# A two-layer hybrid decoder trunk: transposes kept together, up blocks taken two at a time, and the first loads and last stores on two queues

## The chip, the cores and the metric

The kernel runs on one NeuronCore of a Trainium2 chip. The core has a matrix engine (TensorE, PE in the profile, with its weight loads as PEld), a vector engine (VectorE, DVE), a scalar engine (ScalarE, ACT), a general engine (GpSimd, POOL) and a sequencer that only issues transfers (SyncE, SP). Each runs its own stream of instructions in order; semaphores tie the streams together. Matrix results land in PSUM, eight banks of 128 x 512 float32, and DVE or ACT take them from there to SBUF. Transfers between HBM and SBUF are issued by an engine's sequencer onto a queue and carried by 16 DMA engines.

The metric is the device time of one execution in microseconds; lower is better. Timed runs give a median, and one further execution is profiled.

## What is computed

Two layers. In each, a normalised copy of the tokens (256 x 1024) is projected, eight heads of sparse attention and eight heads of forgetting attention run side by side, their result is projected back, and a squared-ReLU MLP follows. Cut to what matters here:

```python
for l in range(DEPTH):                                   # DEPTH = 2
    h = _rms_norm(x, g_pre_mix[l])
    parts = jnp.split(h @ w_in[l], split_at, axis=-1)    # 1024 -> 2848 columns
    o_nsa = _nsa_mixer(...)                              # 8 heads, three branches
    o_fox = _fox_mixer(...)                              # 8 heads
    mix = jnp.concatenate([o_nsa, o_fox], axis=-1) @ w_out[l]
    x = x + _rms_norm(mix, g_post_mix[l])
    h = _rms_norm(x, g_pre_mlp[l])
    y = jnp.square(jax.nn.relu(h @ w_up[l])) @ w_down[l]  # 1024 -> 4096 -> 1024
    x = x + _rms_norm(y, g_post_mlp[l])
```

## The kernel before

**Products in three parts.** A float32 product is made of three products of rounded halves: each operand is split into `hi` (rounded to the type float32r) and `lo` (the rest), and hi*hi, hi*lo and lo*hi are summed in one PSUM bank (`mm3`, L657). The weights come from HBM as float32 into a buffer `wraw` (tag `raw`, 9 buffers), ACT makes `whi` from it and DVE `wlo` (`Weights.get`, L485; 7 buffers of each). So each weight tile of 512 KB costs one load, one ACT instruction and one DVE instruction, and then feeds PE.

**Transposes.** PE also turns blocks of 128 x 128 by a product with the identity (`ident`, a column range of the tile `cst`). These are plain float32. The profile shows them as `s<-cst,...`: `pr` are attention probabilities (`probs_T`, L1215), `mg` the normalised tokens (`to_xT`, L694), `kS` and `kW` keys (`k_transpose`, L865), `h` the first MLP block (`turn`, L1450). Each group of three or four writes one bank with the tag `s`; there are three such banks, two each with the tags `x` and `acc`, and one with the tag `o`.

**Small-tile stretches.** Some attention products use a part of the PE array: the forgetting scores (`s<-fkT,fqT` and `s<-cum,selr`, 64 rows), probability times value (`o<-prT,...`, 64 columns) and the hidden layer of the compressed keys (32 columns). They are recorded inside `nc.stretch()`, which makes one unit of several matmuls.

**The order is planned.** `body` does not issue instructions as the code runs. A `Recorder` collects every operation with its buffers, dependencies and an estimated cost (`_cost`, L446; `_latency`, L423). `order` (L282) then makes a list schedule, five times with due times worked out from the last one, keeps the one that ends first by its own estimate, and `emit` issues the instructions in that order. All instructions thus carry the line L404 in the profile, and groups are told apart by tile names. Outside a stretch the planner is free to put other matmuls between two transposes of one group; inside a stretch it is not. An operation on `sync` counts as a transfer in these estimates (L271, L368, L424, L451).

**The MLP.** Layer by layer, `up(fc)` (L1403) makes 512 of the 4096 hidden columns, transposed, in four blocks `b` of 128. For each block, eight matmuls with `whi` as the stationary operand read 512 columns (both halves of the tokens `xT`, tile `xT[2]`), then eight with `wlo` read 256 columns (the half `xT[0]`), all into one bank of tag `s`. ACT copies the second half of the bank to `h`, DVE adds the first half, and after every second block the squared ReLU is taken and split into the two halves of `aT`. `up` runs for `fc` 1 to 7 in each layer (14 times in all); each is followed by the `down` products of the block before (four weight tiles, 48 matmuls into banks `x` and `acc`). `up0` (L1431) makes the first block in another layout.

**The beginning.** The first eight loads (L598 to L611) each bring one tile `first`: 128 rows with 256 columns of the transposed tokens and 512 of the first weights, 384 KB (388 KB with the gains in front of the first). All are issued by SyncE. `ACT_TABLE_LOAD` (L517) is ACT's first instruction. For each `k`, ACT scales the tokens to `xT` and rounds the weights to `whi` (DVE for `k` = 0), DVE makes both `lo` parts, and PE does six matmuls of 512 columns into the two banks `x`. Before the first load lands, PE runs four warm-up matmuls (`o<-warm`).

**The end.** `sandwich` (L710) of each token tile `t` normalises the down product and adds it to `X[t]`, in two halves of 512 columns; in the last layer each half is stored by SyncE as soon as DVE has written it (L748).

Of the kernel before, what the change touches and what calls it, by code (L numbers as in the profile page):

```python
# [24 lines left out]
P = 128  # L25
D = 1024
S = 256
# [150 lines left out]
class Recorder:  # L178
# [75 lines left out]
    def deadlines(self, out):  # L254


        due, t = {}, 0.0
        for op in out:
            if op.engine == "tensor":
                due[op], t = t, t + op.cost  # L260
        taker = {}
        for q in self.fifo.values():
            for a, b in zip(q, q[q[0].bufs:]):
                taker[a] = b
        first = {}
        for op in out:
            for b in op.bufs:
                first.setdefault(b, op)
        for op in reversed(out):
            d = due.get(op, t)  # L270
            cost = op.cost + LANDING if op.engine == "sync" else op.cost  # L271
            for x in op.succs:
                if x.deps[op] > -1e8 and x in due:
                    d = min(d, due[x] - x.deps[op] - cost)
            for b in op.bufs:
                if taker.get(b) in first and first[taker[b]] in due:
                    d = min(d, due[first[taker[b]]] - (260 if b.psum else 150) - cost)
            due[op] = d
        for op in out:
            op.rank = op.key if op.engine == "tensor" else due[op]  # L280
# [16 lines left out]
    def schedule(self):  # L297
# [41 lines left out]
        while events:  # L339
            t, _, released = heapq.heappop(events)  # L340
            if released is not None:
                free[released] += 1
            if events and events[0][0] == t:
                continue
            for e, ops in waiting.items():
                while busy[e] <= t:
                    best = None
                    for op in ops:
                        if op.ready <= t and (best is None or (best.urgent, -best.rank) < (op.urgent, -op.rank)) and fits(op):
                            best = op  # L350
                    if best is None:
                        break
                    if not best.urgent and e != "tensor" and not force:
                        q = hot[e]
                        while q and q[0].start is not None:
                            q.popleft()
                        memo = {}
                        if any(estimate(op, memo) < t + WAIT * best.cost for op in list(q)[:4] if op.start is None and fits(op)):
                            break
                    ops.remove(best)  # L360
                    for b in best.bufs:
                        if b not in live:
                            live.add(b)
                            free[b.tag] -= 1
                            head[b.tag] += 1
                    best.start = t
                    out.append(best)
                    if e == "sync":  # L368
                        busy[e] = t + 450
                        bus = max(bus, t + 1150) + best.cost  # L370
                        best.end = bus + 900 + LATE
                    else:
                        busy[e] = best.end = t + best.cost
                        if e == "tensor" and best.tile != tiled:
                            busy[e] = best.end = best.end + (tiled == (P, P)) * ENTER + (tiled != (P, P)) * LEAVE
                            tiled = best.tile
                    count += 1
                    heapq.heappush(events, (busy[e], count, None))
                    for b in best.bufs:
                        left[b] -= 1  # L380
                        if not left[b]:
                            count += 1
                            heapq.heappush(events, (best.end + (260 if b.psum else 150), count, b.tag))
                    for s in best.succs:
                        s.ready = max(s.ready, t, best.end + s.deps[best])
                        s.missing -= 1
                        if not s.missing:
                            waiting[s.engine].append(s)
                            count += 1
                            heapq.heappush(events, (s.ready, count, None))  # L390
            force = not events and len(out) < len(self.ops)
            if force:
                heapq.heappush(events, (t + 100, 0, None))
# [27 lines left out]


def _latency(a, b):  # L423
    if a.engine == "sync":  # L424
        return 50.0
    if a.engine == b.engine == "tensor":
        return 0.0
    if a.engine == "tensor":
        return 360.0 if b.name == "tensor_tensor_reduce" else 200.0
    if b.engine == "tensor":  # L430
        return 260.0 if a.engine == "vector" else 230.0
    return 130.0 if a.engine == "vector" else 145.0
# [13 lines left out]
def _cost(op, views):  # L446
# [1 line left out]
    out = op.args[0] if op.args else op.kw["out"]  # L448
    n = int(np.prod(out.shape[1:]))
    part = 100 * (out.shape[0] < P)  # L450
    if op.engine == "sync":  # L451
        v = views[0][1]
        return v.shape[0] * int(np.prod(v.shape[1:])) * 4 / 360.0
    if op.engine == "tensor":
# [68 lines left out]
def trunk(nc, A, consts_in, out, sbp, pp):  # L523
# [6 lines left out]
    def small(shape, name, bufs=2):  # L530
        return tile(shape, F32, name=name, tag=name, bufs=bufs)
# [50 lines left out]
    def weight(*key):  # L582
        return W.get(index[key])
# [13 lines left out]
    for k in range(8):  # L597
# [6 lines left out]
        o = 0 if k else 8  # L604
        f = f[:, 0:o + NFIRST]
        a = 8 + k * NFIRST - o
        nc.sync.dma_start(f, A["first"][:, a:a + o + NFIRST])
        if k == 0:
            gcol0 = f[:, 0:8]
        xTk.append(f[:, o:o + S])  # L610
# [83 lines left out]
    def to_xT(t, n, xg, xT):  # L694

        ps = psum("s")
        for k in range(4):
            nc.tensor.transpose(ps[:, k * P:k * P + P], xg[:, k * P:k * P + P], ident)
        split(ps.rearrange("p (k n) -> p k n", k=4), [y[:, 4 * n:4 * n + 4, t * P:t * P + P] for y in xT[:2]])

    def pre_gain(g_post, g_next):
# [8 lines left out]
    def sandwich(t, acc, g_post, pre=None, xT=None, eps=EPS, store=None):  # L710
# [32 lines left out]
        for n in range(2):  # L743
            if pre:
                m[n] = times("m", n, g_post)
            nc.vector.scalar_tensor_tensor(X[t][:, half(n)], m[n], r, X[t][:, half(n)],
                                           op0=OP.mult, op1=OP.add)
            if store is not None:  # L748
                nc.sync.dma_start(store[:, half(n)], X[t][:, half(n)])
        yield  # L750

    def rope(dst, src, t, nh):
# [31 lines left out]
    for l in range(DEPTH):  # L784
# [80 lines left out]
        def k_transpose(br, src):  # L865

            ps = psum("s")
            for g in range(2):
                for t in range(NT):
                    nc.tensor.transpose(ps[:, g * S + t * P:g * S + t * P + P], src[t][:, g * P:g * P + P], ident)  # L870
            split(ps.rearrange("p (g n) -> p g n", g=2), [y[:, :, br, :] for y in kx])


# [340 lines left out]

        def probs_T(p, eng, e):  # L1215
            ps = psum("s")
            for a in (0, 128, 256):
                nc.tensor.transpose(ps[:, a:a + P], p[:, a:a + P], ident)
            kind, pair, par, br = e
            if kind == "nsa" and pair % 2:  # L1220

# [180 lines left out]

        def up(fc, then=None):  # L1403
            a = [tile([P, 4, S], F32R, name="aT", tag=f"act{j}", bufs=2) for j in range(2)]
            for b in range(4):
                hi, lo = weight(l, "up", fc, b)

                ps = psum("s")
                for k in range(8):
                    nc.tensor.matmul(ps, hi[:, k, :], xT[2][:, k].rearrange("p j n -> p (j n)"), start=k == 0, stop=False,  # L1410
                                     skip_group_check=True)
                for k in range(8):
                    nc.tensor.matmul(ps[:, S:], lo[:, k, :], xT[0][:, k, :], start=False, stop=k == 7,
                                     skip_group_check=True)
                if then is not None and b == 1:
                    then()
                if b % 2 == 0:
                    h = tokt("h")
                d = h[:, (b % 2) * S:(b % 2) * S + S]
                nc.scalar.activation(d, ps[:, S:], AF.Copy)  # L1420
                nc.vector.tensor_add(d, ps[:, :S], d)
                if b % 2:
                    rl = small([P, 512], "rl")
                    nc.scalar.activation(rl, h, AF.Relu)
                    nc.vector.tensor_mul(h, rl, rl)
                    d = [y[:, b - 1:b + 1, :].rearrange("p b n -> p (b n)") for y in a]
                    nc.scalar.activation(d[0], rl, AF.Square)
                    nc.vector.tensor_sub(d[1], h, d[0].bitcast(F32))
            return a

        def up0():  # L1431
# [127 lines left out]
```

## Time and profile before

| | us |
|---|---|
| median of 3 runs (lowest, highest) | 623.21 (622.92, 623.8) |
| the profiled execution, whole time | 622.97 |
| its span, first to last instruction | 621.0 |
| PE busy in it | 613.3 |
| DVE busy | 476.3 |
| ACT busy | 376.3 |

The span lies 2.0 us below the time of its own execution. The mean granted TensorE clock of the profiled run was 0.999 of full speed. A row of the timeline gives the start of a group, how long it lasted from its first start to its last end, the engine, the line, the operation, what is written from what, and the count. Matmuls overlap in a pipeline, so the time that one takes of the engine is the distance to the start of the next, not its own duration. Rows of the chain of waits give the start, the length and the instructions of a piece of the work that ended last.

### The profile page before, as it was taken

The page shows a single profiled execution, that of the slowest core. Times are in us where ns is not written, and L with a number is a line of the kernel's source. Part 1 is how long each engine was busy: PE and PEld are TensorE (multiplying, and loading weights), DVE is VectorE, ACT ScalarE, POOL GpSimd, SP SyncE. Part 2 cuts the span into 40 slices and gives each one's busy share as a digit, 9 for nine tenths or more (in the row PEclk, how much of TensorE's full clock was granted, in tenths as well). Part 3 has the DMA queues.
Part 4 walks back from the last instruction along what each step waited for, and adds up shares of the span by engine and source line. Part 5 has one row for each costly group of instructions (what it writes and reads, how often), then busy time and mean ns, then how long its engine had stood idle before and what let it go on. Part 6 is the DMA issues. An engine that isn't in the chain of part 4 may idle for free.

```text
span 621.0 us, 9923 instructions
## 1 busy us (share of the span) xinstructions
PE 613.3 (99%) x3572; PEld 518.0 (83%) x3572; DVE 476.3 (77%) x1043; ACT 376.3 (61%) x730; POOL 0.2 (0%) x4
## 2 busy tenths in 40 slices
PE   9999999999999999999999999999999999999995
PEld 6989987788888888888888998777888888888884
DVE  6889999789966567566698999987997666566544
ACT  7866777577655455555476758774766555556432
POOL 0000000000000000000000000000000000000000
PEclk9999999999999999999999999999999999999999
DMA  8987636218665546654347793521485556556001
GB/s 317 403 311 277 257 111 218 73 41 306 245 199 203 195 177 201 203 172 135 111 128 255 269 332 103 174 98 69 132 306 204 175 196 196 193 183 202 12 1 68
DMA packets 33600, 115.69 MB, mean 186 GB/s; under 512 B 3984, under 2 KB 4112, under 8 KB 33552
## 3 DMA queue, kind: packets, MB, share of 16 engines
q1 hardware_dynamic: 33552, 115.06, 53.4%
q8 instruction: 28, 0.46, 0.3%
q14 instruction: 20, 0.16, 0.1%
HBM read 114.00 MB, written 1.05 MB: 185 GB/s over the span
## 4 chain that ended last, share of the span: by engine, by line
PE 99%; DVE 0%; issue 0%; DVEq 0%; ACT 0%
PE s L404 35%; PE acc L404 31%; PE x L404 25%; PE o L404 7%; DVE x L404 0%; DVE m L404 0%; DVEq L1555 0%; DVE rsqrt L404 0%; DVE warm L404 0%; ACT rl L404 0%; DVEq L404 0%
## 5 line engine op out<-in xcount | busy, mean ns | idle before, releaser
L404 DVE TENSOR_TENSOR wlo<-wraw,whi 128x1024 fp32r<-128x1024 f32 (+1 forms) x188 | 224.8, 1201 | 80.5 <-ACT whi L404 78.6
L404 ACT ACTIVATE whi<-wraw 128x1024 fp32r<-128x1024 f32 (+1 forms) x188 | 194.8, 1040 | 122.1 <-PE acc L404 72.8
L404 PE MATMUL s<-xT,whi 128*128 128x512 f32 x448 | 112.0, 392 | 0.0
L404 PEld LDWEIGHTS s<-xT,whi 128*128 128x128 f32 x448 | 81.4, 189 | 15.2
L404 PE MATMUL acc<-whi,aT 128*128 128x512 f32 x256 | 88.6, 390 | 0.0
L404 PE MATMUL x<-whi,aT 128*128 128x512 f32 x256 | 88.4, 390 | 0.0
L404 PEld LDWEIGHTS s<-xT,wlo 128*128 128x128 f32 x448 | 61.1, 190 | 4.4
L404 PE MATMUL s<-xT,wlo 128*128 128x256 f32 x448 | 62.5, 282 | 0.0
L404 PEld LDWEIGHTS acc<-whi,aT 128*128 128x128 f32 x256 | 48.1, 188 | 9.9
L404 PEld LDWEIGHTS x<-whi,aT 128*128 128x128 f32 x256 | 48.1, 188 | 9.7
L404 ACT ACTIVATE pr<-pr,st 128x256 f32<-128x256 f32 (+1 forms) x96 | 42.8, 448 | 15.2 <-DVE st L404 14.7
L404 PE MATMUL x<-wlo,aT 128*128 128x512 f32 x128 | 50.0, 390 | 0.0
L404 PE MATMUL acc<-wlo,aT 128*128 128x512 f32 x128 | 49.9, 390 | 0.0
L404 PE MATMUL acc<-xT,whi 128*128 128x256 f32 x256 | 49.7, 288 | 0.0
L404 PEld LDWEIGHTS acc<-xT,whi 128*128 128x128 f32 x256 | 40.2, 190 | 1.6 <-issue 0.4
L404 PE MATMUL acc<-whi,xT 128*128 128x512 f32 (+1 forms) x128 | 38.8, 361 | 0.0
L404 ACT ACTIVATE rl<-h 128x512 f32<-128x512 f32 x28 | 17.7, 632 | 32.5 <-DVE h L404 32.5
L404 PE MATMUL acc<-xT,wlo 128*128 128x256 f32 x128 | 36.6, 286 | 0.0
L404 PE MATMUL x<-whi,xT 128*128 128x512 f32 x112 | 36.3, 397 | 0.0
L404 DVE TENSOR_TENSOR h<-rl 128x512 f32<-128x512 f32 x28 | 19.2, 691 | 16.1 <-ACT rl L404 16.1
L404 PEld LDWEIGHTS acc<-wlo,aT 128*128 128x128 f32 x128 | 24.0, 188 | 5.0
L404 PEld LDWEIGHTS x<-wlo,aT 128*128 128x128 f32 x128 | 24.1, 188 | 4.5
(221 smaller groups left out, 961.9 us busy)
## 6 DMA issues: line engine op xcount, KB each, us to landing
wraw<-in_w_up_dram SPq DMA_DIRECT2D x64, 512.0 KB, 4.2
wraw<-in_w_down_dram SPq DMA_DIRECT2D x64, 512.0 KB, 3.5
wraw<-in_w_in_dram SPq DMA_DIRECT2D x36, 512.0 KB, 4.9
wraw<-in_w_out_dram SPq DMA_DIRECT2D x16, 512.0 KB, 7.7
w<-in_cmp_w_k_dram SPq DMA_DIRECT2D x8, 512.0 KB, 5.8
w<-in_cmp_w_v_dram SPq DMA_DIRECT2D x8, 512.0 KB, 5.3
first<-in_first_dram SPq DMA_DIRECT2D x7, 384.0 KB, 5.9
wraw<-in_w_in_dram SPq DMA_DIRECT2D x8, 288.0 KB, 4.2
```

Of the source, the lines that this page charges most:

```text
L404: getattr(getattr(self.nc, op.engine), name)(*[real(v) for v in args], **{k: real(v) for k, v in kw.items()})
```

## The change

Four things change, and one in the planner that goes with them.

1. The transposes of `to_xT`, `k_transpose` and `probs_T` are recorded inside `nc.stretch()`, so that the three or four of a group stand together and start when all that they read is there.
2. In `up`, blocks go by two: both weights are taken, then come the 16 matmuls with `whi` (eight into each of two banks), then the 16 with `wlo`, then the evacuation of both banks.
3. The first two loads (`k` 0 and 1) are each cut into rows 0 to 63, issued by SyncE, and rows 64 to 127, issued by ACT.
4. The last half of the last token tile is written by DVE in two pieces of 320 and 192 columns; ACT's queue stores the first, SyncE's the second.
5. The planner knows a transfer by its name instead of by its engine.

```diff
-            cost = op.cost + LANDING if op.engine == "sync" else op.cost
+            cost = op.cost + LANDING if op.name == "dma_start" else op.cost
...
-        nc.sync.dma_start(f, A["first"][:, a:a + o + NFIRST])
+        if k < 2:
+            for q, h in ((nc.sync, slice(0, HD)), (nc.scalar, slice(HD, P))):
+                q.dma_start(f[h], A["first"][h, a:a + o + NFIRST])
+        else:
+            nc.sync.dma_start(f, A["first"][:, a:a + o + NFIRST])
...
-        for k in range(4):
-            nc.tensor.transpose(ps[:, k * P:k * P + P], xg[:, k * P:k * P + P], ident)
+        with nc.stretch():
+            for k in range(4):
+                nc.tensor.transpose(ps[:, k * P:k * P + P], xg[:, k * P:k * P + P], ident)
...
-            nc.vector.scalar_tensor_tensor(X[t][:, half(n)], m[n], r, X[t][:, half(n)],
-                                           op0=OP.mult, op1=OP.add)
-            if store is not None:
-                nc.sync.dma_start(store[:, half(n)], X[t][:, half(n)])
+            for a, b in ((0, 512),) if store is None or t == 0 or n == 0 else ((0, 320), (320, 512)):
+                d = X[t][:, n * 512 + a:n * 512 + b]
+                nc.vector.scalar_tensor_tensor(d, m[n][:, a:b], r, d, op0=OP.mult, op1=OP.add)
+                if store is not None:
+                    (nc.scalar if a == 0 and b < 512 else nc.sync).dma_start(store[:, n * 512 + a:n * 512 + b], d)
...
-            for b in range(4):
-                hi, lo = weight(l, "up", fc, b)
-                ps = psum("s")
-                for k in range(8):
-                    nc.tensor.matmul(ps, hi[:, k, :], xT[2][:, k].rearrange("p j n -> p (j n)"), start=k == 0, stop=False,
-                                     skip_group_check=True)
-                for k in range(8):
-                    nc.tensor.matmul(ps[:, S:], lo[:, k, :], xT[0][:, k, :], start=False, stop=k == 7,
-                                     skip_group_check=True)
+            for b in (0, 2):
+                ws = [weight(l, "up", fc, b + i) for i in range(2)]
+                two = [psum("s") for _ in range(2)]
+                for ps, (hi, _) in zip(two, ws):
+                    for k in range(8):
+                        nc.tensor.matmul(ps, hi[:, k, :], xT[2][:, k].rearrange("p j n -> p (j n)"), start=k == 0,
+                                         stop=False, skip_group_check=True)
+                for ps, (_, lo) in zip(two, ws):
+                    for k in range(8):
+                        nc.tensor.matmul(ps[:, S:], lo[:, k, :], xT[0][:, k, :], start=False, stop=k == 7,
+                                         skip_group_check=True)
```

The stretches of `k_transpose` and `probs_T` look like the one of `to_xT`; the evacuation in `up` is the same as before, for the two banks of a pair one after the other. The tests for a transfer in `schedule`, `_latency` and `_cost` change as the one shown.

More of the change, by code (lines that the diff above doesn't have):

```diff
@@ L367, in schedule @@
                     out.append(best)
-                    if e == "sync":
+                    if best.name == "dma_start":
                         busy[e] = t + 450
@@ L423, in _latency @@
 def _latency(a, b):
-    if a.engine == "sync":
+    if a.name == "dma_start":
         return 50.0
@@ L450, in _cost @@
     part = 100 * (out.shape[0] < P)
-    if op.engine == "sync":
+    if op.name == "dma_start":
         v = views[0][1]
@@ L867, in k_transpose @@
             ps = psum("s")
-            for g in range(2):
-                for t in range(NT):
-                    nc.tensor.transpose(ps[:, g * S + t * P:g * S + t * P + P], src[t][:, g * P:g * P + P], ident)
+            with nc.stretch():
+                for g in range(2):
+                    for t in range(NT):
+                        nc.tensor.transpose(ps[:, g * S + t * P:g * S + t * P + P], src[t][:, g * P:g * P + P], ident)
             split(ps.rearrange("p (g n) -> p g n", g=2), [y[:, :, br, :] for y in kx])
@@ L1216, in probs_T @@
             ps = psum("s")
-            for a in (0, 128, 256):
-                nc.tensor.transpose(ps[:, a:a + P], p[:, a:a + P], ident)
+            with nc.stretch():
+                for a in (0, 128, 256):
+                    nc.tensor.transpose(ps[:, a:a + P], p[:, a:a + P], ident)
             kind, pair, par, br = e
@@ L1404, in up @@
             a = [tile([P, 4, S], F32R, name="aT", tag=f"act{j}", bufs=2) for j in range(2)]
-            for b in range(4):
-                hi, lo = weight(l, "up", fc, b)
-                ps = psum("s")
-                for k in range(8):
-                    nc.tensor.matmul(ps, hi[:, k, :], xT[2][:, k].rearrange("p j n -> p (j n)"), start=k == 0, stop=False,
-                                     skip_group_check=True)
-                for k in range(8):
-                    nc.tensor.matmul(ps[:, S:], lo[:, k, :], xT[0][:, k, :], start=False, stop=k == 7,
-                                     skip_group_check=True)
-                if then is not None and b == 1:
-                    then()
[L1417 to L1428, printed above, removed]
@@ new lines, in up @@
+            for b in (0, 2):
[9 more added lines that the diff above has]
+                                         skip_group_check=True)
+                if then is not None and b == 0:
+                    then()
+                h = tokt("h")
+                for i, ps in enumerate(two):
+                    d = h[:, i * S:i * S + S]
+                    nc.scalar.activation(d, ps[:, S:], AF.Copy)
+                    nc.vector.tensor_add(d, ps[:, :S], d)
+                rl = small([P, 512], "rl")
+                nc.scalar.activation(rl, h, AF.Relu)
+                nc.vector.tensor_mul(h, rl, rl)
+                d = [y[:, b:b + 2, :].rearrange("p b n -> p (b n)") for y in a]
+                nc.scalar.activation(d[0], rl, AF.Square)
+                nc.vector.tensor_sub(d[1], h, d[0].bitcast(F32))
```

## The prediction

> **What bounds the kernel now.** I read the page first (busy time, then the shares of the chain of waits), then the chain in order of time, then the timeline of PE where the change touches it.
>
> ```profile
> PE 613.3 (99%) x3572; PEld 518.0 (83%) x3572; DVE 476.3 (77%) x1043; ACT 376.3 (61%) x730; POOL 0.2 (0%) x4
> ...
> PE 99%; DVE 0%; issue 0%; DVEq 0%; ACT 0%
> ```
>
> PE is busy for 99% of the span and makes 99% of the chain, DVE and ACT for 77% and 61%. Waits of ACT and DVE elsewhere cost nothing unless they grow into PE. A gain can come from three places: what PE loses when it changes the kind of its work, the time before its first product, and the time after its last.
>
> The pitch of a matmul is read from the distance of starts:
>
> ```profile
> 166.01 11.15 PE s L404 x64
> ...
> 178.54 1.36 PE acc L404 x6
> 179.90 1.36 PE x L404 x6
> ```
>
> Six matmuls of 512 columns take 179.90 - 178.54 = 1.36 us, 0.2267 each, with no gap. One up block series (64 matmuls) takes 11.15.
>
> **The up blocks.** The four blocks of one series, eight with `whi`, eight with `wlo`, and again:
>
> ```profile
> 165.85 1.98 PE L404 MATMUL s<-xT,whi 128*128 128x512 f32 x8
> 167.66 1.12 PE L404 MATMUL s<-xT,wlo 128*128 128x256 f32 x8
> 168.61 2.00 PE L404 MATMUL s<-xT,whi 128*128 128x512 f32 x8
> 170.45 1.12 PE L404 MATMUL s<-xT,wlo 128*128 128x256 f32 x8
> ```
>
> The first eight, behind other 512-column work, take 167.66 - 165.85 = 1.81 = 8 x 0.2267. The next eight, behind 256-column work, take 170.45 - 168.61 = 1.84: a turn from 256 to 512 columns costs 0.02 to 0.03. Each series has four such turns (the last into the down products); pairs leave two. 14 series x 2 x 0.02 = 0.56 us is taken, 0.84 at the upper end, 0 if what costs is the count of matmuls and not the turn.
>
> Pairs also hold two of the three `s` banks at once. The third block takes the free bank; the fourth needs the first one back. Between the first block's last `wlo` matmul and the fourth block's first matmul PE has 8 x 0.12 (the second `wlo` group) + 1.81 (the third block) = 2.77 us of work. What emptying a bank takes:
>
> ```profile
> 190.67 2.00 PE L404 MATMUL s<-xT,whi 128*128 128x512 f32 x8
> 190.88 0.37 ACT L404 ACTIVATE h<-s 128x256 f32<-128x256 f32 x1
> 191.00 1.23 DVE L404 TENSOR_TENSOR wlo<-wraw,whi 128x1024 fp32r<-128x1024 f32 x1 [0.59 <-ACT whi L404]
> 192.15 0.42 DVE L404 TENSOR_TENSOR h<-s,h 128x256 f32<-128x256 f32 x1
> ```
>
> The block before ends at 190.67 as seen by the next one's start; the bank is empty at 192.57, 1.9 us later, although DVE's add stands behind a whole `wlo`. In the built order of the changed kernel the add again stands behind one `wlo`. So 0.9 us is spare and I take nothing for it; without that cover see the rivals.
>
> **The transposes.** Alone between 512-column matmuls, and four groups with single matmuls between:
>
> ```profile
> 45.66 1.07 PE L404 MATMUL s<-cst,q_tok 128*128 128x128 f32 x8
> 46.49 0.71 PE L404 MATMUL x<-kx,qS 128*128 128x512 f32 x2
> ...
> 134.21 0.39 PE L404 MATMUL s<-whi,xT 128*128 128x512 f32 x1
> 134.44 0.38 PE L404 MATMUL s<-cst,mg 128*128 128x128 f32 x2
> 134.58 0.48 PE L404 MATMUL s<-whi,xT 128*128 128x512 f32 x1
> ...
> 136.95 0.40 PE L404 MATMUL s<-wlo,xT 128*128 128x512 f32 x1
> ...
> 139.91 0.39 PE L404 MATMUL o<-whi,xT 128*128 128x512 f32 x1
> 140.14 0.60 PE L404 MATMUL s<-cst,h 128*128 128x128 f32 x4
> ...
> 141.51 0.39 PE L404 MATMUL o<-wlo,xT 128*128 128x512 f32 x1
> ```
>
> A transpose takes (46.49 - 45.66) / 8 = 0.104. From 139.91 to 141.51 stand five matmuls and four transposes: 1.60 - 5 x 0.2267 - 4 x 0.104 = 0.05 for one separate run. From 134.21 to 136.95 stand eight matmuls and eight transposes in four runs: 2.74 - 8 x 0.2267 - 8 x 0.104 = 0.09. So the first run costs 0.05 and each further one, a single matmul away, 0.015.
>
> The built orders give the counts: 119 runs of transposes before, 85 after; of 34 fewer, 30 were a single matmul from the next one. That is 30 x 0.015 + 4 x 0.05 = 0.65 us gained. Against it, transposes that stood next to a small-tile stretch do so at 13 places before and 7 after, matmuls of full size take the six others, and that side is dearer:
>
> ```profile
> 97.15 0.27 PE L404 MATMUL s<-cst,pr 128*128 128x128 f32 x1
> 97.35 0.93 PE L404 MATMUL s<-fkT,fqT 64*128 64x128 f32 x8
> ...
> 98.39 0.44 PE L404 MATMUL s<-cst,pr 128*128 128x128 f32 x2
> 98.58 0.48 PE L404 MATMUL x<-wlo,oT 128*128 128x512 f32 x1
> ...
> 106.63 0.40 PE L404 MATMUL x<-wlo,oT 128*128 128x512 f32 x1
> 106.96 0.93 PE L404 MATMUL s<-fkT,fqT 64*128 64x128 f32 x8
> ...
> 108.33 0.27 PE L404 MATMUL s<-cst,pr 128*128 128x128 f32 x1
> ```
>
> Between transposes the same scores leave 98.58 - 97.15 - 3 x 0.104 = 1.12, between matmuls 108.33 - 106.63 - 2 x 0.2267 = 1.25: 0.065 a side, 6 x 0.065 = 0.4 lost. Sum -0.25 us. The ends are -1.7 (all 34 at 0.05) and +0.4 (no run gains). A stretch also starts only when its last input is there. In `to_xT` four transposes then follow the second piece of DVE instead of two, 0.2 us later for `xT`; the matmuls between cover it, and the built order places them so. The PE work between a head's scores and its transposes is at least as long in the new order as in the old (smallest 2.84 us in both).
>
> **The head.** Loads, ACT, and the first products:
>
> ```profile
> 0.73 1.28 ACT L517 ACT_TABLE_LOAD   x1 [0.73 <-PEq L1549]
> 0.73 3.82 SPq L404 DMA_DIRECT2D first<-in_first_dram  x8
> ...
> 4.29 0.51 ACT L404 ACTIVATE xT<-first 128x256 fp32r<-128x256 f32 x1 [2.28 <-DMA first<-in_first_dram]
> ...
> 5.62 0.63 ACT L404 ACTIVATE whi<-first 128x512 fp32r<-128x512 f32 x1 [0.82 <-DMA first<-in_first_dram]
> 6.15 0.49 ACT L404 ACTIVATE xT<-first,gcol 128x256 fp32r<-128x256 f32 x1
> ...
> 4.86 0.58 PE L404 MATMUL x<-whi,xT 128*128 128x512 f32 x1
> ...
> 6.70 9.86 PE x L404 x42
> ```
>
> ACT waits for the first tile to 4.29 and the second to 5.62; PE starts at 4.86, and its six products of `k` = 0 (1.36) leave it waiting from 6.22 to 6.70. From there 42 matmuls run without a gap (9.86, of which the last overlaps). So the second tile's landing sets the head. The most to win is 6.70 - 6.22 = 0.48, and 0.1 more at 4.86. Eight issues take 3.82, 0.48 each: with halves on two queues the second tile's issue starts about that much earlier, but the bytes ahead of it stay. I take -0.3, between 0 and -0.6 if ACT issues at once. ACT's two issues stand behind its table load. If they wait for it, the upper half is issued at 2.01 instead of 0.73; with the 3.56 from that issue to ACT's start at 4.29, ACT starts at 5.57, PE (0.57 later) at 6.14, and after 1.36 is at the second tile at 7.5 instead of 6.70: +0.8.
>
> The Trainium skill (DMA: Bandwidth & Descriptors, Issuing engines are not separate DMA queues) says that transfers from both queues run on the same 16 engines and only the sequencer's issue time is saved. By that alone head and tail would give at most their issue times, and with nothing for either the sum is 622.4. No row here shows ACT's queue.
>
> **The tail.** Last updates and stores:
>
> ```profile
> 616.64 1.41 DVE L404 SCALAR_TENSOR_TENSOR x<-m,rsqrt,x 128x512 f32<-128x512 f32 x2
> ...
> 612.04 6.37 SPq L404 DMA_DIRECT2D out_dram<-x  x4
> ...
> wraw<-in_w_down_dram SPq DMA_DIRECT2D x64, 512.0 KB, 3.5
> ...
> out_dram<-x SPq DMA_DIRECT2D x4, 256.0 KB, 2.1
> ```
>
> The last store is issued at 618.1 (612.04 + 6.37 less its own 0.33) and lands 2.1 later; the rest of the span is the close. DVE's two updates take 0.7 each; cut in 320 and 192 the second takes about 0.1 more (an extra start), so the last issue is at 618.2, but carries 96 KB instead of 256. What 160 KB fewer are worth no row shows: the two sizes of the rows above (loads against stores) differ by 1.4 for 256 KB, 0.9 for 160, the far end, and the extra start alone is +0.1, the other. The bytes of the two stores before go ahead of the last ones, so I stay near the small end: -0.15.
>
> **Sum.** -0.56 - 0.25 - 0.3 - 0.15 = -1.26. Against the profiled execution's 622.97 that is 621.7; its time is 0.24 below the median of 623.21, which becomes 621.95, so 622.0.
>
> **Rivals.**
> - *Each run of transposes costs 0.05, and the head is won whole.* For it: the 0.05 measured once; against it: the 0.015 beside it. -0.84 - 1.7 + 0.4 - 0.6 - 0.3 = -3.0: 620.2.
> - *ACT's issues wait for the table load.* For it: both stand in one stream; against it: an issue is the sequencer's, not the engine's, as SP's 0.48 shows. -0.56 - 0.25 + 0.8 - 0.15 = -0.2: 623.0. The Trainium skill (ScalarE: Activation LUTs, What ACT_TABLE_LOAD costs) adds a drain of 1380 ns to the load of 1283, which the row's 1.28 confirms; no row here shows the drain, and with it the time would be 624.4.
> - *The pair runs out of banks (slower).* If ACT's copy or DVE's add stands behind one `whi` and one more `wlo` (1.06 + 1.22), emptying takes 1.9 + 2.3 = 4.2, which is 1.4 above the 2.77; 14 series give +20, less 1.26: 642. It decides from 0.9 us of delay on. Against it is the built order, with one `wlo` only.
> - *Nothing moves:* the turns are the pipeline's own, the adjacency of stretches is lost, head and tail are bound by bytes: 0 to +0.4, 623.4.
>
> **How the numbers follow.** The forecast gets 0.50, the first rival 0.22, the table load 0.14, the banks 0.05, nothing 0.09. 0.2% of 623.21 (1.25 us) is about what a measurement of this kernel can tell from no change. The forecast lies on that bound: half of it is faster, half the same. Faster 0.25 + 0.21 = 0.46; the same 0.25 + 0.10 + 0.06 = 0.41; slower 0.04 + 0.05 + 0.04 = 0.13. The range reaches from the first rival's side (620.4) over the table load with some of a further wait (624.0); the forecast's own is 621.4 to 622.6.
>
> **What would show it.** After the change a series of 64 in the chain takes 11.11 instead of 11.15; a bank wait would show as a gap ahead of the second or fourth group of `whi` matmuls. The piece of the chain that starts at 6.70 starts near 6.4 if the head gains, past 7 if ACT's issue waited, and ACT's issue rows stand at 0.8 or at 2.0. The attention stages keep their length within 0.3 us. The last landing comes 0.1 to 0.2 closer behind PE's last matmul. The prediction is wrong if a stage of attention becomes longer by more than 1 us, or a new wait of PE for ACT or DVE appears.

## The result and the profile after

| | before | after |
|---|---|---|
| median of 13 runs, us (lowest, highest) | 623.31 (622.92, 623.80) | 624.66 (624.11, 625.19) |
| the profiled execution, whole time | 622.97 | 624.81 |
| its span | 621.0 | 623.0 |

The changed kernel is slower: the ratio is 1.0021, its 95% interval 1.0014 to 1.0028. That is 1.35 us at the medians, 2.0 between the two profiled spans. PE is still the bound, as the page after says (its busy line, then the chain of waits by engine):

```profile
PE 614.4 (99%) x3572; PEld 519.9 (83%) x3572; DVE 472.5 (76%) x1044; ACT 381.7 (61%) x730; POOL 0.2 (0%) x4
...
PE 98%; DMA 1%; DVE 0%; issue 0%; DVEq 0%; ACT 0%
```

So the question is at which places PE's stream of matmuls came later or earlier. The chain of waits after, in order of time (start, length, what):

```profile
5.56 13.19 PE x L404 x48
18.75 1.32 PE acc L404 x10
...
145.68 5.98 PE s L404 x36
...
168.14 11.11 PE s L404 x64
```

and the rows of before that stand beside them:

```profile
16.56 1.18 PE acc L404 x9
...
143.51 6.69 PE s L404 x39
```

The reader compares distances. From the first piece of `acc` products to the start of the MLP are 143.51 - 16.56 = 126.95 us before and 145.68 - 18.75 = 126.93 after: all the transposes of the first layer's attention moved by 0.02. A series of 64 takes 11.11 instead of 11.15, as forecast. But that piece starts 2.19 later. The whole loss is in the first 19 us, and the series win back 14 x 0.04 = 0.56 of it.

The tail, after (timeline of DVE and of the transfers, then the list of transfers: engine, count, size, us from issue to landing):

```profile
618.27 1.54 DVE L404 SCALAR_TENSOR_TENSOR x<-m,rsqrt,x 128x512 f32<-128x512 f32 x3
...
613.67 6.50 SPq L404 DMA_DIRECT2D out_dram<-x  x4
...
out_dram<-x ACTq DMA_DIRECT2D x1, 160.0 KB, 2.1
out_dram<-x SPq DMA_DIRECT2D x1, 96.0 KB, 2.1
```

The updates take 1.54 instead of 1.41: the cut costs DVE 0.13. The store of 96 KB lands 2.1 us after its issue, as the 256 KB of before did. So the cut adds 0.13 and the smaller store gives nothing back.

The head, after (timeline; a row gives start, length, engine, what, and in brackets the idle time before it and who ended it):

```profile
0.72 1.28 ACT L517 ACT_TABLE_LOAD   x1 [0.72 <-PEq L1560]
0.76 1.45 ACTq L404 DMA_DIRECT2D first<-in_first_dram  x2
1.18 3.78 PE L404 MATMUL o<-warm 128*128 128x256 f32 x8 [1.18 <-DVE warm L404]
...
5.56 1.20 PE L404 MATMUL x<-whi,xT 128*128 128x512 f32 x2 [0.60 <-DVE gcol L404]
...
6.55 1.05 PE L404 MATMUL x<-wlo,xT 128*128 128x512 f32 x2
...
7.23 0.63 ACT L404 ACTIVATE whi<-first 128x512 fp32r<-128x512 f32 x1 [1.74 <-DMA first<-in_first_dram]
7.41 2.12 PE L404 MATMUL x<-whi,xT 128*128 128x512 f32 x4
...
8.30 0.50 PEld L404 LDWEIGHTS x<-whi,xT 128*128 128x128 f32 x2 [0.56 <-ACT xT L404]
...
9.93 0.86 PE L404 MATMUL x<-whi,xT 128*128 128x512 f32 x3
...
10.63 0.39 PE L404 MATMUL x<-wlo,xT 128*128 128x512 f32 x1
```

Three things are to be seen.

- ACT's two issues stand at 0.76, inside the table load. They did not wait for it.
- ACT waits for the second tile to 7.23 (before: 5.62), and PE loads its first weights at 8.30 (before: 6.70). Both are 1.6 later.
- The two `wlo` products that start at 6.55 have their successor at 7.41: 0.43 us each. The three from 9.93 on have theirs at 10.63: 0.23 each. Up to about 9.5 PE works at half its rate. The windows view does not tell this. Its columns are the window, its length, the busy time and count of PE, PEld, DVE, ACT and POOL, the granted clock, the DMA share and GB/s, and the clock is 1.00 there:

```profile
7.00:8.00 1.00, 1.00 (x4) 0.65 (x2) 0.11 (x1) 0.77 (x2) 0.00 (x0) 1.00 1.02 396
```

That 1.00 is not a reading. The view takes off only what a clock record of the trace withholds, and the first such record of this execution, of the full clock, begins at 9.62 us; ahead of it there is none. So in the view the half rate is in the distance of starts alone, and the place where the records begin says when it ended (all traces are compared under the warm-up matmuls).

### The profile page after: what moved, and what is told of

It reads as the page before. It is cut to its first block, busy times and chain, and to the rows that moved or that the text cites. A ratio compares the mean times of both kernels' runs of the same rounds, so it can differ in the third digit from the quotient of the medians.

```text
span 623.0 us, 9944 instructions
## 1 busy us (share of the span) xinstructions
PE 614.4 (99%) x3572; PEld 519.9 (83%) x3572; DVE 472.5 (76%) x1044; ACT 381.7 (61%) x730; POOL 0.2 (0%) x4
## 4 chain that ended last, share of the span: by engine, by line
PE 98%; DMA 1%; DVE 0%; issue 0%; DVEq 0%; ACT 0%
PE s L404 35%; PE acc L404 31%; PE x L404 26%; PE o L404 7%; DMA first<-in_first_dram 1%; DVE x L404 0%; DVE m L404 0%; DVE rsqrt L404 0%; DVEq L1566 0%; DVE whi L404 0%; ACT rl L404 0%; DVE gcol L404 0%; DVEq L404 0%; ACT L517 0%
## 5 line engine op out<-in xcount | busy, mean ns | idle before, releaser
L404 PE MATMUL s<-xT,whi 128*128 128x512 f32 x448 | 106.5, 390 | 0.0
L404 PEld LDWEIGHTS s<-xT,whi 128*128 128x128 f32 x448 | 83.4, 188 | 16.8
L404 PEld LDWEIGHTS s<-xT,wlo 128*128 128x128 f32 x448 | 57.4, 191 | 2.2
L404 PE MATMUL s<-xT,wlo 128*128 128x256 f32 x448 | 58.1, 283 | 0.0
L404 PE MATMUL acc<-whi,xT 128*128 128x512 f32 (+1 forms) x128 | 37.5, 353 | 0.0
L404 ACT ACTIVATE h<-s 128x256 f32<-128x256 f32 x56 | 21.2, 378 | 16.0 <-PE s L404 16.0
L404 ACT ACTIVATE rl<-x 128x512 f32<-128x512 f32 x24 | 14.7, 611 | 21.8 <-PE x L404 16.6
```

The lines of the kernel that those rows point to most:

```text
L404: getattr(getattr(self.nc, op.engine), name)(*[real(v) for v in args], **{k: real(v) for k, v in kw.items()})
```

## The experiments

Twelve kernels were run in three groups; each is compared with runs of the kernel before on the same chip. In all of them the planner knows a transfer by its name, as in the changed kernel, except in the one with three warm-up matmuls, which is the kernel before with that number changed.

**The groups without loads and stores.** The changed kernel with before's first loads (the edit shown) and before's last stores:

```diff
-        if k < 2:
-            for q, h in ((nc.sync, slice(0, HD)), (nc.scalar, slice(HD, P))):
-                q.dma_start(f[h], A["first"][h, a:a + o + NFIRST])
-        else:
-            nc.sync.dma_start(f, A["first"][:, a:a + o + NFIRST])
+        nc.sync.dma_start(f, A["first"][:, a:a + o + NFIRST])
```

> The grouped transposes and the up blocks by two, with loads and stores as before. If the loss of the change lies in its first two loads: first product at 4.86 us as before, its end of chunk 0 near 16.4, series of 64 up matmuls 11.11 each, and a time 0.4 to 0.8 us below the kernel before (622.5 to 622.9). If the loss lies in the new order of the work: above the kernel before, about 624.

Measured: 622.61 us against 623.06, ratio 0.9991 (0.9982 to 1.0000). The groups are a small gain, with an interval that reaches 1.0000; what made the changed kernel slower is in its head or its tail.

**The head alone.** The kernel before with only the first two loads cut and shared.

> The kernel before with only the first two loads cut into halves on two queues. If the loss lies there: first product near 5.6, the third tile's products late as in the changed kernel, and 2.0 to 2.3 us over the kernel before (625.3 to 625.6). If the loss came from the order of the work: within 0.3 us of the kernel before.

Measured: 625.18 us, ratio 1.0031 (1.0020 to 1.0041), 2.1 us at the medians. The head alone makes the loss. Its timeline of PE:

```profile
5.67 0.71 PE L404 MATMUL x<-whi,xT 128*128 128x512 f32 x2 [1.08 <-DVE gcol L404]
...
8.27 0.74 PE L404 MATMUL x<-whi,xT 128*128 128x512 f32 x2 [0.79 <-ACT xT L404]
```

PE waits twice: to 5.67 for the first tile, and 0.79 more to 8.27 for the second. In this execution PE was at full rate already, and the second tile alone makes it 8.27 - 6.70 = 1.57 late.

**Halves on one queue, whole tiles on two queues.** Two ways to take the cut apart from the sharing:

```diff
# halves, all on SyncE
+            for q, h in ((nc.sync, slice(0, HD)), (nc.sync, slice(HD, P))):
...
# whole tiles, the second on ACT's queue
+        (nc.scalar if k == 1 else nc.sync).dma_start(f, A["first"][:, a:a + o + NFIRST])
```

> The same four half loads, all issued by SyncE. If it is the sharing of the queues that costs: each issue takes at most the 0.39 to 0.45 us of a whole tile, the second tile is there near 5.6 and the time is within 0.6 us of the kernel before. If it is the cutting into halves (more issues, smaller loads): the second tile lands near 7.1 and the loss is 2 us as with two queues.

> The first two loads whole, the second one on ACT's queue. If it is the sharing that costs: the issues of SyncE and ACT that run at the same time take 0.57 us or more instead of 0.39 to 0.45, the second tile lands past 6.2, and 1 to 2 us are lost. If it is the halves: the second tile lands at 5.6 or earlier and nothing is lost, or up to 0.5 us is gained.

Measured: halves on one queue 625.07 us, ratio 1.0035 (1.0022 to 1.0049). Whole tiles on two queues 625.10, ratio 1.0024 (1.0013 to 1.0035), but in two groups: three runs at 623.43 to 623.54 and four at 625.10 to 625.62, with nothing between. The cut is enough to lose; the second queue isn't needed for it. But sharing whole tiles lost as much in four of seven runs, where the expectation had all runs lose or none. In its profiled execution, of the lower group, the second tile lands at 5.23 instead of 5.59, but the first at 4.98 instead of 4.26, and PE is idle ahead of its first product:

```profile
5.58 0.72 PE L404 MATMUL x<-whi,xT 128*128 128x512 f32 x2 [0.83 <-DVE gcol L404]
```

What an issue costs on ACT's queue, in the views of the tile `first` (shortest, median and longest in ns, then the first and last start): a whole tile in the kernel with whole tiles, then the two halves in the changed kernel:

```profile
L404 ACTq DMA_DIRECT2D first<-in_first_dram x1: 396/396/396, 0.8 to 0.8; - x1
```

```profile
L404 ACTq DMA_DIRECT2D first<-in_first_dram x2: 579/712/844, 0.8 to 1.4; - x2
```

On one and the same queue the whole tile is issued in 0.40 us, and neither half in less than 0.58. On SyncE's queue the first issue of all takes 0.39 us in the kernel before and 0.57 with halves on one queue. The comparison holds for the first issues only: farther back in the queue whole tiles took 0.43 to 0.71 us too.

**The cut by columns.** The first two tiles in two loads of all 128 rows each, on SyncE.

```diff
+            for c in (slice(0, S + o), slice(S + o, o + NFIRST)):
+                nc.sync.dma_start(f[:, c], A["first"][:, a + c.start:a + c.stop])
```

> The kernel before, with the first two loads cut by columns (token columns, then weight columns), each part with all 128 rows, all four on SyncE's queue. Theory A (a load of 64 rows is the dear one: 0.57 to 0.60 us to issue, and slower to stream): each part is issued in 0.39 to 0.45 us, the third tile's issue starts near 2.5 us instead of 3.25, and the head loses at most half of what the cut by rows lost: 0 to +0.9 us on the end. Theory B (every further load costs the head, whatever its shape): the loss is the +1.8 us (ratio 1.003) of the cut by rows.

Measured: 624.16 us, ratio 1.0014 (1.0005 to 1.0023), about half of the other's loss, as theory A has it. The median issue took 432 ns again. But the time alone does not show that the rows make the difference. ACT's waits for the first and the second tile, by columns (first fence) and by rows on one queue (second):

```profile
4.20 0.51 ACT L404 ACTIVATE xT<-first 128x256 fp32r<-128x256 f32 x1 [2.19 <-DMA first<-in_first_dram]
6.74 0.63 ACT L404 ACTIVATE whi<-first 128x512 fp32r<-128x512 f32 x1 [2.03 <-DMA first<-in_first_dram]
```

```profile
4.90 0.51 ACT L404 ACTIVATE xT<-first 128x256 fp32r<-128x256 f32 x1 [2.89 <-DMA first<-in_first_dram]
6.72 0.63 ACT L404 ACTIVATE whi<-first 128x512 fp32r<-128x512 f32 x1 [1.32 <-DMA first<-in_first_dram]
```

The second tile is equally late, 1.1 behind the 5.62 of before, whatever the shape of the cut. Only the first tile differs: by columns it comes as before, by rows 0.6 later. That leaves PE idle for 0.52, and in this execution at half rate to about 9.5, while by columns it had its full rate from 6.6 on.

**Pairs alone, transposes alone, tail alone.** The kernel before with one part of the change each.

> The kernel before with the up blocks by two and nothing else (the planner's item with it). Theory (the turn from 256 to 512 columns costs 0.02 us): the series of 64 take 11.11 instead of 11.15 us, the MLP of each layer is 0.28 us shorter, the end 0.56 us earlier, ratio 0.9991. Rival (the 0.56 us seen with both groups belong to the transposes): no change here.

> The kernel before with the grouped transposes and nothing else (the planner's item with it). Theory from the marks (what the runs of transposes gain, the lost neighbours of small-tile stretches give back): 0 on the last matmul's start, between -0.1 and +0.1 us. The prediction's term: -0.25 us. Rival (the groups lose by starting later): +0.2 us or more in the attention stages.

> The kernel before with the cut of the last half token tile and its two stores on two queues, nothing else. Theory (a store takes about 2.07 us from issue to landing whatever its size, and the cut costs DVE one more start): the last landing is 0.1 to 0.2 us further behind PE's last matmul, end +0.16 us, ratio 1.0003. The prediction's term: -0.15 us. Rival (bytes set the last landing): -0.3 us or more.

Measured, against 623.20: the pairs 622.44, ratio 0.9990 (0.9981 to 0.9999); the transposes 623.16, ratio 1.0002 (0.9993 to 1.0011); the tail 623.42, ratio 1.0004 (0.9995 to 1.0013). The pairs give what was forecast, and their median is the lowest of all kernels here, below both the kernel before and the changed one. The transposes give nothing. The tail's +0.2 is not clear of nothing, since its interval holds 1; its trace shows the 0.13 on DVE again, 1.54 against 1.41.

Why grouping gives nothing is seen where three transposes stand as one and two in the kernel before (first fence) and together in the one with groups (second):

```profile
74.78 0.27 PE L404 MATMUL s<-cst,pr 128*128 128x128 f32 x1
74.81 0.48 PE L404 MATMUL acc<-whi,xT 128*128 128x512 f32 x1
75.13 0.38 PE L404 MATMUL s<-cst,pr 128*128 128x128 f32 x2
75.26 0.48 PE L404 MATMUL acc<-wlo,xT 128*128 128x512 f32 x1
75.58 0.40 PE L404 MATMUL acc<-whi,xT 128*128 128x512 f32 x1
```

```profile
75.11 0.49 PE L404 MATMUL s<-cst,pr 128*128 128x128 f32 x3
75.36 0.48 PE L404 MATMUL acc<-wlo,xT 128*128 128x512 f32 x1
75.68 0.39 PE L404 MATMUL acc<-whi,xT 128*128 128x512 f32 x1
```

Apart: 75.58 - 74.78 = 0.80, less two matmuls of 0.2267, leaves 0.347. Together: 75.68 - 75.11 = 0.57, less one matmul, leaves 0.343. A further run costs 0.004 here, less than the 0.01 to which rows are given.

**Warm-up matmuls.** The two groups of times of the whole tiles on two queues asked for a cause that is there or not from one execution to the next. The half rate of PE in the head is such a cause. Theory C says: PE gets its full rate only after it has been busy for a full stretch of time; the changed loads leave it idle between its warm-up and its first product, and then some executions have to wait for a further stretch. Three kernels test it with the number of warm-up matmuls (`WARM`, L41), which touches no load:

```diff
-WARM = 4
+WARM = 5    # whole tiles on two queues; the changed kernel
...
-WARM = 4
+WARM = 3    # the kernel before
```

> The kernel with the first two loads whole, one on each queue, and five warm-up matmuls instead of four, so that PE has work until the first product. Theory C (PE runs at half rate until it has been busy for a full stretch; the idle time ahead of the later first product lets some executions miss it): the upper group of 625.1 to 625.6 us disappears, every run lies between 623.2 and 623.9, no product of 512 columns behind the first four takes 0.43 us. Theory L (the two groups come from how the loads land): both groups stay.

> The changed kernel with five warm-up matmuls instead of four. Theory C: products run at 0.23 us from the third or fourth on; the second tile still sets the head (its first product near 8.3 us instead of 6.7), so the loss of the head goes from +2.2 to +1.6 us and the median from 624.7 to 624.1 us, with all runs below 624.4. Theory L (loads alone): no change, 624.7 us, products at 0.43 us until 9.5 us.

> The kernel before with three warm-up matmuls instead of four: no load is touched, PE is idle from about 3.9 us to its first product near 4.9. Theory C: products at 0.43 us for a further stretch in most executions, some up to 9.5 us, time +0.5 to +2 us, in groups. Theory L: no change, 623.1 us.

Measured: the whole tiles on two queues with five 623.64 us, ratio 1.0009 (1.0000 to 1.0018), eleven runs from 623.51 to 624.18: the upper group is gone. Three runs lie above the 623.9 expected, none above 624.2.

The kernel before with three: 624.85 us, ratio 1.0019 (1.0009 to 1.0028), seven of ten runs at 624.64 to 625.19 and three at 622.91 to 623.79. One warm-up matmul less, with the loads as they were, costs about as much as the whole change (ratio 1.0019 against 1.0021). Its timeline of PE:

```profile
1.18 2.93 PE L404 MATMUL o<-warm 128*128 128x256 f32 x6 [1.18 <-DVE warm L404]
4.88 1.21 PE L404 MATMUL x<-whi,xT 128*128 128x512 f32 x2 [0.77 <-DVE gcol L404]
5.89 1.05 PE L404 MATMUL x<-wlo,xT 128*128 128x512 f32 x2
6.74 1.91 PE L404 MATMUL x<-whi,xT 128*128 128x512 f32 x4
8.45 1.05 PE L404 MATMUL x<-wlo,xT 128*128 128x512 f32 x2
9.30 1.08 PE L404 MATMUL x<-whi,xT 128*128 128x512 f32 x3
```

PE is idle for 0.77 us, has its first tile at 4.88 as before, and then makes products at 0.43 ((8.45 - 6.74) / 4) until some time after 9.30. Theory L, that the loads alone count, falls.

The changed kernel with five: 624.17 us, ratio 1.0017 (1.0009 to 1.0026), against 624.66 with four. The medians differ by 0.5 as expected (0.4 when each is taken against its own runs of before), but the two intervals overlap, and two of its eleven runs (624.62 and 625.12) lie above the 624.4 expected. What the trace shows is plain:

```profile
1.18 4.63 PE L404 MATMUL o<-warm 128*128 128x256 f32 x10 [1.18 <-DVE warm L404]
...
8.81 0.73 PE L404 MATMUL x<-whi,xT 128*128 128x512 f32 x2 [1.24 <-ACT xT L404]
9.38 0.62 PE L404 MATMUL x<-wlo,xT 128*128 128x512 f32 x2
9.84 0.84 PE L404 MATMUL x<-whi,xT 128*128 128x512 f32 x3
```

PE is at full rate ((9.84 - 9.38) / 2 = 0.23), and waits 1.24 for the second tile. So there are two losses: the second tile is late whatever PE's rate, and the half rate comes on top of it. This execution took 624.62 us, one of the two above 624.4, without any half rate: its second tile let ACT start at 7.73 only, against 7.23 in the changed kernel and 7.18 with the head alone. The landing varies too.

The clock records bear theory C out in the main. In all fourteen traces the distance of starts of PE's matmuls falls to half where the first record, of the full clock, begins:

| executions | PE idle ahead of its first product, us | the full clock begins at, us |
|---|---|---|
| head alone; whole tiles on two queues; transposes alone; tail alone | 1.08; 0.83; 0.45; 0.15 | 4.07; 4.41; 4.33; 4.47 |
| before; late halves; pairs alone; columns; groups; with five warm-ups the whole tiles and the changed kernel | none | 5.10; 5.31; 6.12; 6.58; 7.20; 5.08; 5.71 |
| halves on one queue; the changed kernel; three warm-ups | 0.52; 0.60; 0.77 | 9.56; 9.62; 9.76 |

Where PE had its full clock before the warm-up ended, idle time did not take it away again. Where it had not, it came by 7.2 if PE went on without a break, and only after 9.5 if there was a break of 0.5 to 0.8 us. The upper group of the whole tiles on two queues was not profiled; that it belongs in the third row is argued, from the table and from its absence with five warm-up matmuls.

**Halves in the middle of the stream.** Tiles five and six cut by rows instead of one and two, to see whether the cut costs only at the start.

> The kernel before with tiles five and six (instead of one and two) cut into two loads of 64 rows each, all on SyncE's queue, where PE is behind the loads. Theory P (loads of 64 rows stream at about half the pace: 1.8 us a tile instead of 0.98, as between the second halves of the first two tiles when all halves were on one queue): tile eight lands 1.5 to 1.8 us later than before's 12.15, near 13.8; PE needs it only near 15, so the time moves by less than 0.4 us. Theory S (only the start is sensitive, the stream is bound by bytes): tile eight lands within 0.4 us of 12.15.

Measured: 624.12 us, ratio 1.0016 (1.0007 to 1.0025). Both time terms were wrong. The cost is 0.9 and not below 0.4; in the profiled execution PE was 0.25 behind by 9.6 us, from its second tile, and lost another 0.7 on the tiles from the fifth on. And tile eight landed at 13.46, 1.31 later than before's 12.15, between the two theories but near P. The stream itself is clear in the windows view, this kernel first and then before (last column GB/s):

```profile
7.00:8.00 1.00, 1.00 (x5) 0.81 (x5) 1.00 (x3) 0.89 (x2) 0.00 (x0) 1.00 1.06 243
8.00:9.00 1.00, 1.00 (x6) 0.82 (x5) 0.61 (x2) 0.41 (x1) 0.00 (x0) 1.00 1.04 243
9.00:10.00 1.00, 1.00 (x6) 0.68 (x4) 0.74 (x2) 0.62 (x2) 0.00 (x0) 1.00 1.04 255
```

```profile
7.00:8.00 1.00, 1.00 (x6) 0.76 (x5) 1.00 (x3) 1.00 (x3) 0.00 (x0) 1.00 1.05 366
8.00:9.00 1.00, 1.00 (x6) 0.83 (x5) 1.00 (x3) 1.00 (x3) 0.00 (x0) 1.00 1.01 406
9.00:10.00 1.00, 1.00 (x6) 0.83 (x5) 1.00 (x3) 1.00 (x3) 0.00 (x0) 1.00 1.04 366
```

While the halves are under way the engines are as busy (share 1.04) and move 243 to 255 GB/s instead of 366 to 406. A load of 64 rows streams at about 0.65 of the pace of one of 128. The trace's transfer records say the same of single packets: one of 3072 bytes took 198 to 221 ns at the median from 7.5 to 10.5 us, and 121 ns in the kernel before. That it is the rows and not the smaller load is seen with the cut by columns: its packets of 2048 bytes took 84 ns and those of 1024 bytes 46, about before's pace by the byte.

## Why the prediction was wrong, point by point

The forecast was 622.0 us, a gain; 624.66 was measured, a loss. The step that failed is the head.

- **Up blocks, -0.56: right, with its mechanism.** The series take 11.11, the pairs alone gave -0.76 at the medians and their interval holds -0.56. No gap stands in the series of 64, so the rival of the banks fell.
- **Transposes, -0.25: nothing came.** The first layer's attention moved by -0.02 in the changed kernel, and the transposes alone gave -0.04 at the medians. The price of a further run was 0.004 where it can be read, not 0.015 or 0.05, so there was hardly anything to gain; and since the sum of gain and loss is near zero, the 0.4 set against the gain did not show either. The forecast had taken the price of a run as a remainder after 0.104 a transpose, a number from a run of eight; such remainders of some hundredths, times 30, made the term.
- **Tail, -0.15: measured +0.13 on DVE and nothing from the size.** It is the end of the range that had the extra start alone. The loads and stores of unlike size, from which the gain of a smaller store was taken, were no measure of it.
- **ACT's issues and the table load: that rival fell.** The issues stand inside the load. ACT waited for its first tile to 4.98 anyway, so no row can show a drain behind the load, and none delayed an issue. That the price with the drain, 624.4, lies near the measured time is chance.
- **Head, -0.3: this is the step that failed.** It ran: "with halves on two queues the second tile's issue starts about that much earlier, but the bytes ahead of it stay", between 0 and -0.6 if ACT issues at once. ACT did issue at once, and the head lost 2.2 in the profiled execution, with a new wait of PE, 0.60 ahead of its first product. At the medians it is an estimated 1.35 + 0.56 - 0.13 = 1.8, and 2.1 with the head alone. There was also less to win than the 0.48 at 6.70 that the prediction took. In the kernel before, the fifth and sixth products of `k` = 0 open this row:

```profile
6.08 1.37 PE L404 MATMUL x<-whi,xT 128*128 128x512 f32 x4
```

They end near 6.08 + 2 x 0.2267 = 6.53, which leaves 0.17. Two things were left out:

- *The halves were costed as if a load were its bytes.* Of the first issues a half took 0.57 us or more, a whole tile 0.38 to 0.42, and the bytes of a half move at 0.65 of the pace. The second tile came 1.6 later, and the prediction itself had found that this tile sets the head. The Trainium skill (DMA: Bandwidth & Descriptors, Issuing engines are not separate DMA queues) says that a second queue saves issue time only; the runs agree that it adds no pace (at most 406 GB/s in the windows of the changed kernel, 409 in those of before, from 2 to 12 us). With halves it did not save issue time for the second tile either: its halves were issued at 1.35 and 1.36, the whole tile of before at 1.17.
- *PE's rate in the head was taken as full.* The prediction reckoned six products at 1.36 from 4.86 on. But a hint stood in a row that it quoted: the product at 4.86 lasts 0.58 us, those in the middle of the kernel 0.39. In the kernel before the warm-up runs into the first product, and the full clock begins at 5.10. With the first product 0.7 later there is a gap, and in the profiled execution the full clock begins at 9.62. That added 2.19 - 1.6 = 0.6 there, and about 0.5 at the medians (624.66 with four warm-up matmuls, 624.17 with five). The two parts are not independent: at half rate the six products of `k` = 0 keep PE to about 8.3, so a second tile on time would have gained next to nothing in this execution, and with three warm-up matmuls the half rate alone costs 1.6.

Why the full clock begins where it does isn't visible in a trace of one execution. The Trainium skill (TensorE: Matmul & The Clock Gate, What's actually happening) has an explanation: PE's clock is halved when idle, is released after one busy window of 3.4 us, and these windows run freely, not from the start of the kernel. Its figures fit: half rate, 512 columns at 1.2 GHz, would be an estimated 0.427 us, and 0.43 was measured. So do the two groups, since where the windows fall changes from run to run, and so do the records: those of the full clock last 614.40 or 610.99 us, which differ by 3.41. One thing fits less well: with the head alone the full clock begins 2.9 us after PE's first matmul, which is less than a whole window. That keeping PE busy decides it is shown by the runs and by the records; how the window counts is not.

Open is why 64 rows stream more slowly, and why the second tile is late when the cut is by columns, with packets at full pace. The runs show the pace and the dearer issue, not what the engines wait for.

## What to carry to other kernels

A load that sets the start should stay whole here: cut by columns or by rows on one queue, the second tile came 1.1 us later, the rows made issue and stream dearer as well, and a second queue did not make up for it. Warm-up work has to reach until the first real product; a change that makes the first data later by 0.7 us can cost more through PE's rate than through the wait (whole tiles on two queues: 623.5 in one group, 625.1 and more in the other). Read the distance of starts there, or where the trace's clock records begin: a clock of 1.00 ahead of the first record says nothing. Take the parts of a change by themselves: here one of four gave the gain (622.44 us with the pairs alone), and the rest took it back.

## What the runs showed of the hardware that was not expected

- PE at half rate (0.43 us for 512 columns instead of 0.23) until the first clock record begins (9.62 us in the changed kernel, 5.10 before), and 0.77 us of idle time ahead of the first product enough to cost a median of 1.6 us (624.85 against 623.21).
- Idle time behind the begin of the full clock left it standing: 1.08 us with the head alone (4.07), 0.83 with whole tiles on two queues (4.41).
- On ACT's queue a load of 64 rows took 0.58 us or more to issue against 0.40 for 128 rows with twice the bytes, and such loads streamed at 243 to 255 GB/s against 366 to 406.
- A store of 96 KB lands no sooner after its issue (2.1 us) than one of 256 KB.
- An issue on ACT's queue runs inside ACT's table load (issues at 0.76 and 1.36 us, the load from 0.72 to 2.00).
